# Feed-forward gate and up products by seven block products instead of eight

## The chip, the cores and the metric

The program runs on one core of one Trainium2 chip. Its time is the device time of one execution in microseconds (us). Engines: PE multiplies matrices (TensorE), ACT is ScalarE, DVE is VectorE, POOL is GpSimd, and SP is SyncE, whose queue issues nearly all DMAs here. PEld is PE's loading of weights, which runs beside its matmuls.

## The reference, cut to what matters

One layer of a hybrid decoder, for 1024 prompt tokens and 32 sample tokens (1056 in all), model width 1024, hidden width 2048, all in float32:

```
x += 1/2 * SwiGLU_1(rms(x))
x += W_out(sig(g_s5) * Up_s5(S5 branch) + sig(g_m) * Up_m(mLSTM branch))
x += 1/2 * SwiGLU_2(rms(x))
x += (p @ W_ple) * sigmoid(rms(x) @ W_ple_gate)
y  = rms(x) * g_final

SwiGLU(x) = (silu(x @ w_gate) * (x @ w_up)) @ w_down     # 1024 -> 2048 -> 1024
```

The change touches the two SwiGLU stages, called FFN1 and FFN2 here, and the places where x enters and leaves them.

## The kernel before, in words

Activations lie with features on the 128 partitions and the 1056 tokens along the free axis: x is 8 tiles of 128x1056. Tokens are taken in three chunks of 384, 384 and 288 (CH, L31), so that an accumulator fits a bank of PSUM. A float32 product is made of three matmuls in the type fp32r. Each factor is split into a high half (ACT rounds it, L87) and the rest (DVE subtracts, L88), and `mm3` (L101 to L106) adds high by high, high by low and low by high. `unit` (L108) is one accumulator: 24 matmuls for 8 feature tiles of 128.

An FFN (`ffn`, L246) goes over 16 tiles of 128 hidden features. For each, `gate_up` (L253) loads a 128-column piece of the gate and of the up weight (512 KB each, `weight`, L90), splits them, and makes three units of each. DVE multiplies the gate's unit by the 1/RMS of its token (`rb`, L262), ACT takes silu, DVE multiplies by `rb` and by the up unit, and the result is split into `hh` and `hl` (L268), which stay on chip. `down` (L270) takes groups of 4, 4, 4, 2 and 2 hidden tiles, with one further `gate_up` put ahead of each group so that PE has work while the last halves are split; its results are added to x on DVE (L279).

The RMS norm is folded: products run on x times gain. `norm` (L161) gives a hook, called once for each tile and chunk of x as it becomes final; the hook makes the two halves of x times gain (ACT L176, DVE L177), and the sums of squares come after it (L197, L198). `rstd` (L203) makes 1/RMS: two small PE products (L218, L235) with a power on POOL (L225) between.

Start of FFN1: `load_x` (L118) loads nine token tiles, transposes each with PE (`xT`, L155), takes it from PSUM on ACT or DVE (L139), and after the tiles 2, 5 and 8 calls the hook for one chunk. So the first chunk's products can begin after three token tiles. Start of FFN2: `join` (L1152) ends with a loop over chunks, and inside it over the 8 tiles (L1182): 6 matmuls (`mm_wo`), DVE's addition to x (L1175), and the hook.

The order of instructions on each engine is written by a scheduler that simulates them; each engine then runs its own list strictly in order, and waits on semaphores of others. Tiles come from pools with a fixed count of buffers (L39 to L49): 3 buffers for high halves of weights and 3 for low, 2 for raw weights, 16 + 8 + 10 large tiles for activations, and 4 + 4 banks of PSUM (`pmm`, `paux`).

Of the kernel before, what the change touches and what calls it, by code (L numbers as in the profile page):

```python
# [30 lines left out]
CH = ((0, 384), (384, 384), (768, 288))   # token chunks of a product  # L31


class Kernel:
    def __init__(self, tc, a, outs, ctx, dbg=None):
# [16 lines left out]
    def consts(self):  # L52
# [55 lines left out]
    def unit(self, w, xs, j, name, c=0, mw=P, aux=False):  # L108
        """One accumulator: products of all feature tiles for token chunk j."""
# [32 lines left out]
    def transpose_in(self, xp, xs, put, nf, name, pool, after=None, loaded=()):  # L142
        """put(feature tile, columns, PSUM tile) takes the tokens, transposed."""
        nc = self.nc
        for t in range(9):
# [4 lines left out]
            else:  # L150
                tt = pool.tile([P, NT if pool is self.ph else RW], F32, tag="h" if pool is self.ph else "r", name=f"{name}in{t}")[:n, :nf * P]
# [51 lines left out]
    def rstd(self, j, ss, rc, rb, name, cols=False):  # L203
        """1 / RMS of token chunk j, refined by one Newton step: columns [token, 128-token tile] and spread over the partitions."""
# [32 lines left out]

    def new_hl(self, n, name, lo="a"):
        lt = lambda k: (self.pa.tile([P, NT], F32R, tag="a", name=f"{name}l{k}") if lo == "a" else
                        self.px.tile([P, XW], F32R, tag="x", name=f"{name}l{k}")[:, :NT])  # L240
        return [(self.pa.tile([P, NT], F32R, tag="a", name=f"{name}h{k}"), lt(k)) for k in range(n)]

    def gate_up_weights(self, wg, wu, name, m):
        return [self.weight(w[:, m * P:(m + 1) * P], f"{name}{q}{m}") for q, w in (("g", wg), ("u", wu))]
# [1083 lines left out]
```

## Time and profile before

| | us |
|---|---|
| timed runs, median of 3 | 2344.37 |
| lowest and highest | 2341.33, 2345.77 |
| profiled execution, span from first to last instruction | 2343.1 |
| PE busy | 2310.0 (99%) |
| DVE busy | 1288.1 (55%) |
| ACT busy | 716.7 (31%) |
| POOL busy | 56.7 (2%) |

For the profiled execution only the span is given; it lies 1.3 us under the median and inside the range of the timed runs. A busy time is the union of an engine's instructions; successive matmuls overlap in the record, so the cost of one in a row of many is the distance from start to start and not its listed duration.

### The profile page before, as it was taken

Reading aid. Unit: us, or ns where it says so; the run is one execution under the profiler, and the core shown is the slowest. Engines: PE = TensorE matmul, PEld = TensorE weight load, DVE = VectorE, ACT = ScalarE, POOL = GpSimd, SP = SyncE. Lnnn points to the kernel's source line nnn. Section 1 sums busy time; section 2 is a strip of 40 time slices with the busy share of each in tenths; the row PEclk is TensorE's granted clock in tenths of the full one; section 3 lists DMA queues with packets and bytes.
Section 4 is the critical chain, followed back from the end, with each engine's and each line's share of the span. In section 5 each row is a group of like instructions: output and inputs, shape, how many; then the busy total and the mean of one; then the engine's idle time right before and its main releaser. Section 6 shows DMA issues by size and latency. Waiting matters only on the chain.

```text
span 2343.1 us, 36797 instructions
## 1 busy us (share of the span) xinstructions
PE 2310.0 (99%) x14895; PEld 2273.2 (97%) x14895; DVE 1288.1 (55%) x3101; ACT 716.7 (31%) x1332; POOL 56.7 (2%) x90
## 2 busy tenths in 40 slices
PE   8999999999999999999999899999999999999999
PEld 7999999999999999999999789999999999999998
DVE  6333333346868866868676377535533333334755
ACT  6111212114434433444344433213311111111543
POOL 0000000000001100000000000000000000000000
PEclk9999999999999999999999999999999999999999
DMA  4111111111444551222223488331111111111111
GB/s 136 39 55 37 55 37 55 46 46 42 141 117 132 138 141 39 60 59 62 52 76 97 138 275 279 100 129 46 55 37 55 36 55 37 55 37 59 56 37 74
DMA packets 254225, 188.37 MB, mean 80 GB/s; under 512 B 27052, under 2 KB 242060, under 8 KB 254056
## 3 DMA queue, kind: packets, MB, share of 16 engines
q1 hardware_dynamic: 234816, 164.43, 24.2%
q10 hardware_dynamic: 19240, 21.59, 2.7%
q8 instruction: 117, 1.92, 0.4%
q14 instruction: 52, 0.43, 0.1%
HBM read 142.09 MB, written 41.40 MB: 78 GB/s over the span
## 4 chain that ended last, share of the span: by engine, by line
PE 92%; DVE 4%; DMA 2%; issue 1%; ACT 1%; SPq 0%; DVEq 0%; ACTq 0%
PE mm_qk L104 3%; PE mm_f2g L105 3%; PE mm_f1g L105 3%; PE mm_qk L106 3%; PE mm_f2g L106 3%; PE mm_f2g L104 3%; PE mm_f2u L104 3%; PE mm_f1g L104 3%; PE mm_f1u L105 3%; PE mm_f1g L106 3%; PE mm_f2u L105 3%; PE mm_qk L105 3%; PE mm_f2u L106 3%; PE mm_f1u L106 3%; PE mm_f1u L104 3%; PE mm_f2d L104 2%
## 5 line engine op out<-in xcount | busy, mean ns | idle before, releaser
L104 PE MATMUL mm_qk<-n2h,wh_qk 128*128 128x384 f32 (+1 forms) x384 | 126.5, 329 | 0.0
L105 PE MATMUL mm_f1g<-n1l,wh_f1g 128*128 128x384 f32 (+1 forms) x384 | 125.9, 328 | 0.2 <-DVE n1l L177 0.2
L104 PE MATMUL mm_f2d<-f2hh,wh_f2d 128*128 128x384 f32 (+1 forms) x384 | 125.7, 327 | 0.3 <-DVE x L279 0.3
L106 PE MATMUL mm_qk<-n2h,wl_qk 128*128 128x384 f32 (+1 forms) x384 | 125.8, 328 | 0.0
L104 PE MATMUL mm_f1g<-n1h,wh_f1g 128*128 128x384 f32 (+1 forms) x384 | 125.5, 327 | 0.0
L105 PE MATMUL mm_f1u<-n1l,wh_f1u 128*128 128x384 f32 (+1 forms) x384 | 125.0, 325 | 0.0
L104 PE MATMUL mm_f1d<-f1hh,wh_f1d 128*128 128x384 f32 (+1 forms) x384 | 124.3, 324 | 0.4 <-DVE x L279 0.4
L104 PE MATMUL mm_f1u<-n1h,wh_f1u 128*128 128x384 f32 (+1 forms) x384 | 124.5, 324 | 0.0
L105 PE MATMUL mm_qk<-n2l,wh_qk 128*128 128x384 f32 (+1 forms) x384 | 124.4, 324 | 0.0
L106 PE MATMUL mm_f1u<-n1h,wl_f1u 128*128 128x384 f32 (+1 forms) x384 | 124.3, 324 | 0.0
L105 PE MATMUL mm_f2g<-n3l,wh_f2g 128*128 128x384 f32 (+1 forms) x384 | 124.2, 323 | 0.0
L106 PE MATMUL mm_f1g<-n1h,wl_f1g 128*128 128x384 f32 (+1 forms) x384 | 124.1, 323 | 0.0
L104 PE MATMUL mm_f2u<-n3h,wh_f2u 128*128 128x384 f32 (+1 forms) x384 | 124.0, 323 | 0.0
L105 PE MATMUL mm_f2d<-f2hl,wh_f2d 128*128 128x384 f32 (+1 forms) x384 | 124.0, 323 | 0.0
L105 PE MATMUL mm_f1d<-f1hl,wh_f1d 128*128 128x384 f32 (+1 forms) x384 | 124.0, 323 | 0.0
L106 PE MATMUL mm_f1d<-f1hh,wl_f1d 128*128 128x384 f32 (+1 forms) x384 | 123.9, 323 | 0.0
L105 PE MATMUL mm_f2u<-n3l,wh_f2u 128*128 128x384 f32 (+1 forms) x384 | 123.9, 323 | 0.0
L106 PE MATMUL mm_f2g<-n3h,wl_f2g 128*128 128x384 f32 (+1 forms) x384 | 123.9, 323 | 0.0
L106 PE MATMUL mm_f2u<-n3h,wl_f2u 128*128 128x384 f32 (+1 forms) x384 | 123.8, 322 | 0.0
L106 PE MATMUL mm_f2d<-f2hh,wl_f2d 128*128 128x384 f32 (+1 forms) x384 | 123.8, 322 | 0.0
L104 PE MATMUL mm_f2g<-n3h,wh_f2g 128*128 128x384 f32 (+1 forms) x384 | 123.6, 322 | 0.0
L279 DVE SCALAR_TENSOR_TENSOR x<-mm_f2d,x 128x384 f32<-128x384 f32 (+1 forms) x120 | 62.5, 523 | 88.8 <-PE mm_f2d L106 88.8
(628 smaller groups left out, 6826.1 us busy)
## 6 DMA issues: line engine op xcount, KB each, us to landing
wr_f1g<-in_w_gate_dram SPq DMA_DIRECT2D x16, 512.0 KB
wr_f1u<-in_w_up_dram SPq DMA_DIRECT2D x16, 512.0 KB
wr_f1d<-in_w_down_dram SPq DMA_DIRECT2D x16, 512.0 KB
wr_qk<-in_w_in_dram SPq DMA_DIRECT2D x16, 512.0 KB
c<-in_state_mlstm_c_dram SPq DMA_DIRECT2D x32, 256.0 KB
out_dram<-c ACTq DMA_DIRECT2D x32, 256.0 KB
wr_f2g<-in_w_gate_dram SPq DMA_DIRECT2D x16, 512.0 KB
wr_f2u<-in_w_up_dram SPq DMA_DIRECT2D x16, 512.0 KB
```

Source lines behind the costliest of these rows:

```text
L104: mm(ps, wh, xh, start=start, stop=False)
L105: mm(ps, wh, xl, start=False, stop=False)
L106: mm(ps, wl, xh, start=False, stop=stop)
L279: nc.vector.scalar_tensor_tensor(xs, ps, 0.5, xs, op0=ALU.mult, op1=ALU.add)
```

## The change

Gate and up are computed for 256 hidden columns at a time (8 steps `u`, each gate then up). The factors are cut into 2x2 blocks: the weight's 256 columns in two halves of 128 and its 8 feature tiles in two interleaved halves of 4 (even and odd tiles); x in even and odd tiles and two token halves of 528 (SH). Strassen's scheme in Winograd's form then needs seven block products, each over 4 feature tiles (12 matmuls), where the plain one needs eight. Each product is run for two column pieces of 264 tokens (SC).

- `forms`: for each pair of x tiles ACT makes x times gain (`fill`), POOL makes four sums or differences of 528 columns, in place over x's own tiles, and seven forms are split on ACT and DVE. 28 forms, each a tile that holds both halves, stay on chip for the whole FFN.
- `sweights`: for each 256 columns two raw loads, four additions on POOL (128x512), seven splits.
- `sproducts`: the seven products of a column piece in four accumulators (a, d from `pmm`, b, c from `paux`); ACT copies one to a temporary, DVE combines them, and `gate` or `up` takes the four blocks of the result. POOL does the multiplications by `rb` and by the gate.
- The hidden tiles are stored to DRAM (`d_h`) and loaded again for the down products, in groups of 8, 6 and 2. Because the forms overwrite x, x is stored to DRAM (`d_xs`) before and loaded again at the down products.
- `load_x` builds the forms after the ninth token tile. The last loop of `join` goes tile by tile instead of chunk by chunk, and the hook builds the forms of a pair when its second tile is final.
- The three pools of large tiles become one of 34, the weights' halves share 8 buffers, raw weights have 3 and the buffer for dynamic DMA descriptors is set to 512.

```
+    def forms(self, i, fill, tmp, name):
+        n = [self.pr.tile([P, RW], ...)[:, :NT] for q in "ab"]
+        fill(i, *n)
+        s = {"b11": n[0][:, :SH], "b21": n[1][:, :SH], "nb22": n[1][:, SH:]}
+        for j, q in enumerate(("t1", "t2", "t3", "t4")):
+            s[q] = tmp[j // 2][:, j % 2 * SH:(j % 2 + 1) * SH]
+        g.tensor_tensor(s["t3"], n[0][:, SH:], s["nb22"], ALU.add)
+        g.tensor_tensor(s["t1"], n[0][:, SH:], s["b11"], ALU.subtract)
+        g.tensor_tensor(s["t2"], s["nb22"], s["t1"], ALU.add)
+        g.tensor_tensor(s["t4"], s["b21"], s["t2"], ALU.add)
+        for q in self.FORMS:
+            f[q] = self.pa.tile([P, 2, SH], F32R, tag="s", name=f"{name}{q}_{i}")
+            self.split(s[q], f[q][:, 0], f[q][:, 1])
...
+    def sweights(self, src, name):
...
+        def form(q, src, add=None):
+            if add is not None:
+                g.tensor_tensor(src, src, add, ALU.add)
+            t = pw.tile([P, 2, 4, P], F32R, tag="w", name=f"w{q}_{name}")
+            self.split(src, t[:, 0], t[:, 1])
+        form("a11", a11)
+        form("s3", a11, a21)
+        form("s2", a11, a22)
+        form("s1", a21, a22)
+        form("a12", a12)
+        form("a22", a22)
+        form("s4", a12, a11)
...
+    def sproducts(self, W, F, c, name, put):
...
+        def product(ps, k, start):
+            for i, f in enumerate(F):
+                for j, (wq, xq) in enumerate(((0, 0), (0, 1), (1, 0))):
+                    nc.tensor.matmul(ps, w[:, wq, i], f[q][:, xq, cs], ...)
+        product(a, 0, True)
+        nc.scalar.copy(p1, a)
+        product(d, 1, True)
+        product(b, 2, True)
+        v.tensor_tensor(v2, b, p1, ALU.add)
+        v.tensor_tensor(w3, d, v2, ALU.subtract)
+        product(e, 3, True)
+        put(1, 1, e, w3, ALU.add)
+        product(a, 4, False)
+        put(0, 0, a, None, None)
+        product(d, 5, False)
+        put(1, 0, d, v2, ALU.subtract)
+        product(e, 6, False)
+        put(0, 1, v2, e, ALU.subtract)
...
+    def norm_s(self, g, name):
...
+        def fill(i, na, nb):
+            nc.scalar.activation(na, xa, AF.Copy, scale=ga)
+            nc.scalar.activation(nb[:, :SH], xb[:, :SH], AF.Copy, scale=gb)
+            nc.scalar.activation(nb[:, SH:], xb[:, SH:], AF.Copy, scale=nb_)
+        def build(i):
+            for m in (2 * i, 2 * i + 1):
+                nc.sync.dma_start(self.d_xs[m], self.x[m])
+            F.append(self.forms(i, fill, self.x[2 * i:2 * i + 2], name))
...
+        groups = ((0, 8), (8, 6), (14, 2))
+        self.x = None
+        for f, n in groups:
+            for m in range(f, f + n):
+                nc.sync.dma_start(h, d_h[m])
+                self.split(h, hh, hl)
+            if not f:
+                for m in range(KT):
+                    nc.sync.dma_start(self.x[m], self.d_xs[m])
...
-            if t in done:
-                for m in range(KT):
-                    hook(m, done[t])
+            if t == 8:
+                for i in range(4):
+                    build(i)
...
-        for j in range(3):
-            for m in range(KT):
+        for m in range(KT):
+            for j in range(3):
                 piece(ws[m // 4], mg[6:], m, m % 4, j)
-                hook(m, j)
+            hook(m)
```

**Place 1: PE at the start of FFN1.** `xT` are the transposes of token tiles, `mm_f1g` and `mm_f1u` the accumulators of gate and up, `n1h` and `n1l` the halves of x times gain. Before, around the last transposes of the third token tile:

```order
L155 MATMUL xT_6_195<-ident,xin_102 128x128
L104 MATMUL mm_f1g_0_492<-n1h_203,wh_f1g_239 128x384
L155 MATMUL xT_7_198<-ident,xin_102 128x128
L104 MATMUL mm_f1u_0_521<-n1h_203,wh_f1u_245 128x384
L155 MATMUL xT_0_251<-ident,xin_249 128x128
L105 MATMUL mm_f1g_0_492<-n1l_204,wh_f1g_239 128x384
L106 MATMUL mm_f1g_0_492<-n1h_203,wl_f1g_240 128x384
```

Now, from the last transpose of the ninth and last token tile (`nrb` spreads 1/RMS; `mma` to `mmd` are the four accumulators, the digit behind the step the column piece, `n1b` and `n1t` forms of x, with the pair's number behind them):

```order
L235 MATMUL xT_7_366<-ident,xin_343 128x32
L315 MATMUL nrb_n_507<-ident,rc_n_100 128x128 x3
L315 MATMUL nrb_n_520<-ident,rc_n_100 128x128 x3
L315 MATMUL nrb_n_535<-ident,rc_n_100 128x128 x2
L315 MATMUL nrb_n_535<-ident,rc_n_100 128x32
L183 MATMUL mma_f1g_0_572<-n1b_0_382,wa_f1g_547 128x264 x3
L183 MATMUL mmd_f1g_0_589<-n1t_0_385,ws_f1g_551 128x264
L183 MATMUL mma_f1g_1_685<-n1b_0_382,wa_f1g_547 128x264 x3
L183 MATMUL mmd_f1g_1_702<-n1t_0_385,ws_f1g_551 128x264
L183 MATMUL mmb_f1g_0_602<-n1t_0_388,ws_f1g_555 128x264
L183 MATMUL mmd_f1g_0_589<-n1t_0_385,ws_f1g_551 128x264 x2
```

Before, products stand between the transposes; now none stands before the last transpose and the spread of 1/RMS, and the first ones take turns over the accumulators as the forms of pair 0 come.

**Place 2: PE at the start of FFN2.** Before, from the end of the last `join` loop into the first gate product:

```order
L104 MATMUL mm_wo_2_2_16572<-mgh_14942,wh_wo_16280 128x288
L105 MATMUL mm_wo_2_2_16572<-mgl_14943,wh_wo_16280 128x288
L106 MATMUL mm_wo_2_2_16572<-mgh_14942,wl_wo_16281 128x288
L104 MATMUL mm_f2g_0_16678<-n3h_16292,wh_f2g_16666 128x384
L105 MATMUL mm_f2g_0_16678<-n3l_16293,wh_f2g_16666 128x384
```

Now, from the place where the sums of squares of the third and last chunk of tokens are taken (`nps`, behind the products that read the last pair's form `n3b_3`):

```order
L183 MATMUL mma_f2g_0_17808<-n3b_3_17714,wa_f2g_17798 128x264 x2
L183 MATMUL mma_f2g_1_17921<-n3b_3_17714,wa_f2g_17798 128x264 x2
L315 MATMUL nrb_n_17752<-ident,rc_n_15980 128x128 x3
L298 MATMUL nps_n_17757<-ones,rb_n_15979 128x2 x2
L298 MATMUL nps_n_17757<-ones,rb_n_15979 32x2
L315 MATMUL nrb_n_17771<-ident,rc_n_15980 128x128 x2
L315 MATMUL nrb_n_17771<-ident,rc_n_15980 128x32
L183 MATMUL mmb_f2g_0_17838<-n3t_0_17414,ws_f2g_17791 128x264 x3
L183 MATMUL mmb_f2g_0_17838<-n3t_1_17512,ws_f2g_17791 128x264 x3
```

Before, the first gate product follows the last `mm_wo` at once, and the norm comes under later products. Now PE's list holds only `mma` and `mmd` products between the last `mm_wo` and the whole norm, and every `mmb` and `mmc` stands behind the norm's last spread.

**Place 3: SP's queue at the change from the products to the down stage of FFN1.** `d_f1h` is the hidden tiles' place in DRAM, `f1hr` a hidden tile loaded again, `wr_f1d` raw down weights, `x_f` x loaded again. None of the stores and reloads has a row before.

```order
L398 DMA f1hr_4535<-d_f1h 128x1056
L100 DMA wr_f1d_5_4993<-in_w_down_dram 128x8x128
L389 DMA d_f1h<-f1h_4014 128x1056
L398 DMA f1hr_4541<-d_f1h 128x1056
L389 DMA d_f1h<-f1h_4013 128x1056
L100 DMA wr_f1d_6_5077<-in_w_down_dram 128x8x128
L398 DMA f1hr_4547<-d_f1h 128x1056
L398 DMA f1hr_4553<-d_f1h 128x1056
L404 DMA x_f_4557<-d_xs 128x1056
```

The stores of the last step's two hidden tiles stand ahead of the reloads of the sixth, seventh and eighth hidden tile, and these ahead of x.

## Rows read from the trace of the kernel before

**Rows 1.** The page's head: span, and busy time, share and instructions of each engine.
```profile
span 2343.1 us, 36797 instructions
...
PE 2310.0 (99%) x14895; PEld 2273.2 (97%) x14895; DVE 1288.1 (55%) x3101; ACT 716.7 (31%) x1332; POOL 56.7 (2%) x90
```

**Rows 2.** The longest of PE's waits: line, releaser: us in total, times, longest.
```profile
PE nnT L1050 <- DVE smA L1047: 9.5, 1, 9.5
```

**Rows 3.** The chain that ended last, share of the span by engine.
```profile
PE 92%; DVE 4%; DMA 2%; issue 1%; ACT 1%; SPq 0%; DVEq 0%; ACTq 0%
```

**Rows 4.** PE's timeline at four moments: start, duration, engine, line, operation.
```profile
199.96 0.34 PE L104 MATMUL mm_f1g<-n1h,wh_f1g 128*128 128x384 f32 x1
...
204.17 0.34 PE L104 MATMUL mm_f1u<-n1h,wh_f1u 128*128 128x384 f32 x1
...
1113.60 0.28 PE L868 MATMUL v2t<-wh_v,n2h 128*128 128x256 f32 x1
...
1115.96 0.28 PE L870 MATMUL v2t<-wh_v,n2l 128*128 128x256 f32 x1
```

**Rows 5.** Work of `mm_f1g`, then `mm_f1u`, in the first 60 us (count in brackets).
```profile
0.00:60.00 60.00, 24.84 (x99) 17.57 (x99) 2.12 (x4) 1.00 0.43 135
...
0.00:60.00 60.00, 21.23 (x89) 16.25 (x90) 1.56 (x3) 1.00 0.43 135
```

**Rows 6.** ACT's instructions by shape: count, busy us, mean ns; then idle time.
```profile
L197 ACT ACTIVATE sq_n<-x 128x384 f32<-128x384 f32 x42 | 21.8, 519 | 7.5 <-DVE ss_n L198 2.9 <-DVE nt_n L227 2.6 <-DVE nt_n L226 1.6
L87 ACT ACTIVATE wh_f1d<-wr_f1d 128x1024 fp32r<-128x1024 f32 x16 | 17.0, 1062 | 63.4 <-PE mm_f1d L105 41.1 <-issue 12.5 <-PE mm_f1g L105 9.9
...
L87 ACT ACTIVATE f1hh<-f1h 128x384 fp32r<-128x384 f32 x32 | 16.8, 526 | 113.7 <-DVE f1h L267 113.7
...
L176 ACT ACTIVATE n1h<-x,vecs 128x384 fp32r<-128x384 f32 x16 | 9.2, 611 | 0.0
...
L126 ACT ACTIVATE junk<-xin 128x1024 f32<-128x1024 f32 x8 | 8.5, 1060 | 2.4 <-DMA xin<-in_x_prompt_dram 2.2
L139 ACT COPY x<-xT 128x128 f32<-128x128 f32 x32 | 7.5, 260 | 6.9 <-PE xT L155 6.9
...
L87 ACT ACTIVATE wh_gt<-wr_gt 128x512 fp32r<-128x512 f32 x1 | 0.6, 634 | 1.8 <-issue 1.8
```

**Rows 7.** DVE's instructions by shape.
```profile
L198 DVE TENSOR_TENSOR ss_n<-ss_n,sq_n 128x384 f32<-128x384 f32 x42 | 23.3, 554 | 0.3
L88 DVE TENSOR_TENSOR wl_f1d<-wr_f1d,wh_f1d 128x1024 fp32r<-128x1024 f32 x16 | 19.6, 1226 | 8.8 <-ACT wh_f1d L87 8.8
...
L1175 DVE SCALAR_TENSOR_TENSOR x<-mm_wo,x 128x384 f32<-128x384 f32 x32 | 17.8, 557 | 31.3 <-PE mm_wo L106 31.3
...
L621 DVE TENSOR_TENSOR s5y<-S,s5x 128x256 f32<-128x256 f32 x8 | 3.4, 420 | 7.3 <-PE S L619 7.3
...
L88 DVE TENSOR_TENSOR wh_gt<-wr_gt,wh_gt 128x512 fp32r<-128x512 f32 x1 | 0.7, 692 | 0.1
```

**Rows 8.** POOL's instructions by shape.
```profile
L225 POOL TENSOR_TENSOR rc_n<-nv_n,mhalf 128x3 f32<-128x3 f32 x12 | 12.7, 1056 | 1423.1 <-DVE nv_n L221 833.9 <-ACT n4h L176 545.0 <-DVE nv_n L224 22.6
L582 POOL TENSOR_TENSOR s5y<-s5c,s5v 128x576 f32<-128x576 f32 x8 | 9.9, 1239 | 103.7 <-DMA s5x<-d_u 64.9 <-ACT s5x L576 14.4 <-DMA s5x<-d_k 12.4
```

**Rows 9.** Stretches: us, busy PE, PEld, DVE, ACT, POOL; PE's clock; DMA share; GB/s.
```profile
0.00:20.00 20.00, 12.81 (x44) 9.47 (x45) 9.95 (x37) 14.37 (x33) 2.86 (x18) 1.00 0.84 287
...
593.00:598.00 5.00, 5.00 (x33) 5.00 (x33) 4.97 (x15) 2.79 (x7) 0.00 (x0) 1.00 1.05 402
...
1330.00:1340.00 10.00, 4.46 (x20) 2.23 (x24) 2.56 (x7) 0.44 (x1) 0.00 (x0) 0.55 0.45 136
...
1630.00:1640.00 10.00, 10.00 (x68) 9.86 (x67) 10.00 (x22) 7.70 (x15) 0.00 (x0) 1.00 0.01 2
```

**Rows 10.** Timelines of POOL and DVE around 738 us.
```profile
737.26 1.22 POOL L582 TENSOR_TENSOR s5y<-s5c,s5v 128x576 f32<-128x576 f32 x1 [2.92 <-ACT s5x L576]
...
738.10 1.47 DVE L88 TENSOR_TENSOR wl_gm<-wr_gm,wh_gm 128x1024 fp32r<-128x1024 f32 x1 [0.76 <-ACT wh_gm L87]
```

More of the change, by code (lines that the diff above doesn't have):

```diff
@@ L81, in vectors @@
         self.gain = {n: vec[:, 8 * i:8 * i + 8] for i, n in enumerate(("g_ffn1", "g_mix", "g_ffn2", "g_ple", "g_mhead"))}
+        neg = pc.tile([P, 2, 8], F32, name="nvecs")
+        for i, n in enumerate(("g_ffn1", "g_ffn2")):
+            nc.vector.tensor_scalar(neg[:, i], self.gain[n], -1.0, None, op0=ALU.mult)
+            self.gain["-" + n] = neg[:, i]
         self.cw = vec[:, 40:104].rearrange("p (j t) -> p j t", j=4)
@@ new lines, in sweights @@
+    def sweights(self, src, name):
+        nc, pw, g, v = self.nc, self.pw, self.nc.gpsimd, self.nc.vector
+        A = []
+        for mh in range(2):
+            raw = pw.tile([P, KT, P], F32, tag="raw", name=f"wr{mh}_{name}", bufs=3)
+            nc.sync.dma_start(raw, src[:, mh * P:(mh + 1) * P].rearrange("(k p) m -> p k m", p=P))
+            A.append([raw.rearrange("p (i k) m -> p k i m", k=2)[:, kh] for kh in range(2)])
+        (a11, a12), (a21, a22) = A
+        out = []
+        def form(q, src, add=None):
[3 more added lines that the diff above has]
+            self.split(src, t[:, 0], t[:, 1])
+            out.append(t)
+        form("a11", a11)
[5 more added lines that the diff above has]
+        form("s4", a12, a11)
+        return out
@@ L122, in load_x @@
+    def load_x(self, build, st):
+        self.x = [self.px.tile([P, XW], F32, tag="s", name=f"x{m}")[:, :NT] for m in range(KT)]
         ss = self.pt.tile([P, 9], F32, tag="ssc", name="ssc", bufs=1)
-        def squares(t, tt):
-            junk = self.pr.tile([P, RW], F32, tag="r", name=f"junk{t}")[:tt.shape[0], :DM]
-            self.nc.scalar.activation(junk, tt, AF.Square, accum_out=ss[:tt.shape[0], t:t + 1])
         def after(t, tt):
@@ L150, in transpose_in @@
             else:
-                tt = pool.tile([P, NT if pool is self.ph else RW], F32, tag="h" if pool is self.ph else "r", name=f"{name}in{t}")[:n, :nf * P]
+                tt = pool.tile([P, XW if pool is self.ph else RW], F32, tag="s" if pool is self.ph else "r", name=f"{name}in{t}")[:n, :nf * P]
                 nc.sync.dma_start(tt, src)
@@ L236, in rstd @@
         nc.scalar.copy(rb[:, o:o + n], ps)
-    def new_hl(self, n, name, lo="a"):
[L239 to L244, printed above, removed]
@@ L292, in down @@
                         hook(m, j)
-        done = 0
-        for i, (f, n) in enumerate(groups):
-            while done < f + n:
-                gate_up(done)
-                done += 1
-            last = i == len(groups) - 1
-            if not last:
-                gate_up(done)
-                done += 1
-            elif before_last:
-                before_last()
-            down(f, n, last)
     def scratch(self):
@@ L849, in head_proj @@
         rb, rc = st["rb"], st["rc"]
-        q, k = ([self.ph.tile([P, NT], F32, tag="h", name=f"{n}{h}_{i}")[:, :NP] for i in range(2)] for n in "qk")
+        q, k = ([self.ph.tile([P, NT], F32, tag="s", name=f"{n}{h}_{i}")[:, :NP] for i in range(2)] for n in "qk")
         for i in range(2):
@@ L1139, in gated_heads @@
         for k in ks:
[L1140 to L1141 removed]
+            hl = [self.pa.tile([P, NT], F32R, tag="s", name=f"hm{q}{k}") for q in "hl"]
             self.hm.append(hl)
[L1143 removed]
+            f1 = self.px.tile([P, XW], F32, tag="s", name=f"hm{k}")[:, :NT]
             f2 = self.pr.tile([P, RW], F32, tag="r", name=f"to{k}")[:, :NT]
@@ L1166, in join @@
                 self.split(t, mg[m][0][:, o:o + n], mg[m][1][:, o:o + n])
-        self.x = [self.pa.tile([P, NT], F32, tag="a", name=f"x2_{m}") for m in range(KT)]
+        self.x = [self.pa.tile([P, NT], F32, tag="s", name=f"x2_{m}") for m in range(KT)]
         for m in range(KT):
@@ L1221, in output @@
         v.tensor_copy(gain, ps)
-        ss = [self.ph.tile([P, NT], F32, tag="h", name=f"fss{j}")[:, :CH[j][1]] for j in range(3)]
+        ss = [self.ph.tile([P, NT], F32, tag="s", name=f"fss{j}")[:, :CH[j][1]] for j in range(3)]
         def hook(m, j):
```

192 lines of the change are left out of this document (120 added, 72 removed).

## The prediction

> **What bounds the kernel now.** I read the page's head first: PE is busy 2310.0 of 2343.1 us, DVE 55%, ACT 31%, POOL 2% [rows 1]. Then PE's waits: only some 33 us of the span are without a matmul, and the longest single wait is 9.5 us, far from the feed-forward stages [rows 2]. The chain of waits says the same: 92% of what ended last is PE [rows 3]. So the time is the number of matmuls times their spacing, and a change pays if it takes matmul columns away and keeps PE fed. The spacing comes from PE's timeline [rows 4]: 24 matmuls of 384 columns lie between 199.96 and 204.17 us, 175.4 ns each, and 20 of 256 columns between 1113.60 and 1115.96 us, 118.0 ns each. That is 0.448 ns for each further column. By interpolation 288 columns cost 132.4 ns and the new 264 columns 121.6 ns. No row has 264 columns; 118.0 and 132.4 bound it.
>
> Two places then decide what else happens: the starts of the two stages. At the first, PE does 188 feed-forward matmuls by 60 us [rows 5]. 144 of them are the six units of hidden tile 0, 24 x (2 x 175.4 + 132.4) ns x 2 = 23.2 us, and 44 more at 175.4 ns are 7.7 us. So 29.1 us of the first 60 are start cost. At the second, PE is busy 10.00 of 10 us from 1630 to 1640 while DVE is full too and ACT is at 7.7 [rows 9]: PE has no idle time there, but the engines that prepare its data have no room.
>
> **The products: what is removed.** Now each FFN makes 32 triples of units, 11.60 us each: 371.1 us. After, it makes 8 steps x gate and up x 2 pieces x 7 products x 12 = 2688 matmuls of 264 columns: 326.9 us. Saved: 44.2 us per FFN, 88.4 us in all. At the bounds of the spacing (118.0 and 132.4 ns) it is 107.8 or 30.4; I keep the interpolation, since both ends lie on one line with 384, and allow 5 us.
>
> **The steady state.** For 256 hidden columns of one weight PE needs 168 x 121.6 ns = 20.4 us. In that time the weight's forms need four additions on POOL and seven splits. POOL's 128x576 addition took 1.239 us [rows 8]; in proportion 512 columns are 1.10 us and 264 are 0.57. A split of 128x512 took 0.634 us on ACT [rows 6] and 0.692 on DVE [rows 7]. For a step u (two weights, 40.9 us) DVE has 14 splits, 9.7 us, and 24 operations on PSUM at about 0.43 (the row with 256 columns has 0.420): 20 us, 49%. ACT has 14 splits and 12 small operations, some 14 us. POOL has 8 additions, 8.8 us, and 20 multiplications, 11.4 us: 20 us, 49%. PE stays the bound; I cost this at nothing. The cover is gone when one weight's chain exceeds 20.4 us (third rival).
>
> **Start of FFN1.** Before, products begin after three token tiles; now after nine and their forms [place 1 of the change]. Until x is complete ACT has 9 squares of 1.06 us, 32 copies of 0.26 and 8 weight splits of 0.634 [rows 6], 23 us after the first landing near 4 us, and SP brings nine token tiles and three raw weights, 5.9 MB, which at 287 GB/s [rows 9] is 20.5 us. With the waits between them I take 33 us (27 to 38). Then ACT alone must make the forms. Its scaled copy of 384 columns took 0.611 us, and from 634 and 1062 ns for 512 and 1024 columns each further column is 0.836 ns: 4 copies of 1056 at 1.17, 8 of 528 at 0.73, 28 splits at 0.65 make 28.7 us; three spreads of `rb` and six weight splits make 5.3; waits for POOL's first sums some 2. The last form is ready near 69 us. PE by then can have done the accumulators of four products as the forms come, about 120 matmuls, 14.6 us. Start cost 54.4 us against 29.1: a loss of 25 (15 to 35).
>
> **Start of FFN2.** From the beginning of the last `join` loop DVE has 24 additions to x (16 at 0.557, 8 at about 0.46), 21 additions of squares (14 at 0.554, 7 at about 0.45), 28 splits of 528 columns at 0.71 and seven weight splits at 0.692 [rows 7]: 12.6 + 10.9 + 19.9 + 4.8 = 48.2 us. ACT has 24 squares (16 at 0.519, 8 at about 0.44), the 12 fills, 28 splits and seven weight splits: 11.8 + 10.6 + 18.1 + 4.4 = 44.9. PE meanwhile has 144 matmuls of `mm_wo`, 23.2 us, and the products into accumulators a and d alone, 72 matmuls, 8.8 us, because its list holds every b and c product behind the norm [place 2]. The norm's tail is a power on POOL, 1.06 us [rows 8], some small steps on DVE, a product and a copy: 4 us after the last sum. 48.2 + 4 - 32.0 = 20 us of idle PE where there was none. Bounds 10 and 30.
>
> **The hidden tiles through DRAM.** The last two are stored only when POOL has multiplied them; SP's queue holds the reloads of the sixth to eighth tile behind these stores [place 3]. Two stores, three reloads (541 KB each) and a weight are 3.2 MB, 8 us at 402 GB/s, the rate of the stores of x now [rows 9]; with 1.2 us on ACT and 1.25 on DVE for the last split (by the 1024-column rows) about 11 us after the last product. PE has the parts of four accumulators that use the first five tiles, 60 matmuls at a mean of 161 ns, 9.7 us. Left: some 3 us per FFN (0 to 12), 6 in all. x comes behind in the same queue; the first addition to x waits for it, and PE then has four banks' worth more. The later groups of 6 and 2 hidden tiles need buffers that the group before frees: 1 us at each of four borders (0 to 3), 4 in all.
>
> **The clock.** From 1330 to 1340 us PE was busy 4.46 of 10 us and its granted clock fell to 0.55 [rows 9], the lower of the levels 1.2 and 2.4 GHz for most of that stretch. Each of the new idle stretches at the starts can cost a few us at the lower level when PE comes back: 4 us (0 to 12).
>
> **The sum.** -88.4 + 25 + 20 + 6 + 4 + 4 = -29 us. The mixer keeps its order around the matmuls; its buffers come from the shared pool, for which I take 0 and allow 10 both ways. Against the profiled execution: 2343.1 - 29 = 2314. The median of the timed runs is 1.3 us higher, so **2315 us**.
>
> **First rival: the starts are hidden better.** If the scheduler's order lets PE eat the forms as they come and both starts together cost 25 instead of 45, and handovers, borders and clock 5 instead of 14, the gain is 58: 2286 us. For it: ACT and DVE work on different forms at once, and PE only needs one pair's forms at a time. Against: both lists are nearly full in my sums, and the b and c products stand behind the norm. Chance 0.20.
>
> **Second rival: POOL and DVE exclude each other.** While POOL's addition ran from 737.26 to 738.48, DVE's split began at 738.10 and took 1.47 us instead of 1.226 [rows 7, 10]: 0.24 us longer for 0.38 us of overlap. If that holds all along, 16 additions of 528 columns (1.14 us, 18 us) and 28 splits (19.9 us) of one FFN go one after the other: 38 us where ACT needs 34 at the first start (4 more), and 48.2 + 18 at the second (18 more). 2315 + 22 = 2337 us. The steady state would still fit: 20 + 9.7 us in 40.9. Against: one overlapping pair is thin, and the additions fall partly into DVE's gaps. Chance 0.13.
>
> The Trainium skill, "SBUF — State Buffer" (section "SBUF: two separate sides"), says that a GpSimd operation and a VectorE operation with two SBUF inputs take the shared ports as an exclusive lock, and the later one blocks fully. By that rule this rival holds; the trace's one pair agrees with it in direction, 0.24 us of 0.38.
>
> **Third rival, slower: a weight's chain is longer than its products.** The seven forms of a weight are made in place, addition and split in turn. Strictly in series that is 4 x 1.10 + 7 x (0.634 + 0.692) = 13.7 us, and POOL's ten multiplications for the same 20.4 us of PE put up to 5.7 between: 19.4. It decides above 20.4. With POOL's and DVE's steps a fifth longer (1.47 for 1.226) the chain is 22.5 to 23.3; half of the excess of 2.9, over 32 weights, is 46 us: 2360 us, the whole of it 2407. For it: POOL goes from 2% to half. Against: eight weight buffers let a chain begin half a step ahead. Chance 0.14.
>
> **Fourth rival: DRAM at the handover.** If the queue's reloads and x are late by the upper bounds, 12 us at each change of stage and 3 at each border, 22 and 8 come instead of 6 and 4, and the clock takes 12: 2315 + 28 = 2343 us, no change that can be told. Chance 0.10.
>
> **How the numbers follow.** My forecast holds with 0.43, from 2300 to 2332 by its own bounds. A measurement of this kernel can tell about 0.2%, 4.7 us, from no change. Faster than 2339.7: 0.43 + 0.20, two thirds of 0.13 and a third of 0.10: 0.75. Within: the rest of the second rival and some of the fourth, 0.08. Slower: the third and the last part of the fourth, 0.17. The range of 8 in 10 goes from 2284 (first rival) into the lower part of the third, 2355.
>
> **What would show it.** Right: matmuls of 264 columns 121 to 122 ns apart; PE's rows in the first 70 us some 25 us emptier than now; 15 to 25 us of waits on DVE or ACT around the end of `mm_wo`; almost no waits of PE in `mma` to `mmd` in between. The second rival would show in splits of 0.71 us stretched towards 1.3 beside POOL; the third in PE waiting for weight forms in each step; the fourth in PE's waits for `f1hh` or in additions to x that wait for DMA. The forecast is wrong if the products' spacing is off the line, if these waits come in every step, or if the starts cost under 30 us or over 65 together.

## The result and the profile after

The changed kernel takes 2326.25 us (median of 4, 2323.53 to 2326.41) against 2345.07 before: ratio 0.9919, 95% interval 0.9905 to 0.9933. It is faster by 19 us where 29 were forecast; the time is inside the range (2284 to 2355) and inside the forecast's own bounds (2300 to 2332), 11 us above the forecast. The profiled execution has a span of 2324.7 us, 18.4 less than [rows 1]. The page's head answers to those rows:

```profile
span 2324.7 us, 39749 instructions
...
PE 2252.8 (97%) x15663; PEld 2206.2 (95%) x15663; DVE 1394.2 (60%) x3211; ACT 823.7 (35%) x1560; POOL 549.1 (24%) x570
...
PE 88%; DVE 6%; DMA 2%; issue 1%; ACT 1%; POOL 1%; SPq 1%; DVEq 0%; ACTq 0%; POOLq 0%
```

PE's busy time fell by 57 us and the span by 18: PE's share of the chain fell from 92% [rows 3] to 88%, DVE's rose from 4% to 6%, and POOL came in with 1%. PE's waits (line, releaser: us, times, longest) say where:

```profile
PE vT L79 <- DMA vrows<-in_conv_b_dram: 8.0, 1, 8.0
PE mma_f2g L183 <- DVE n3b L93: 7.6, 3, 5.2
PE mmd_f1g L183 <- ACT n1t L92: 6.2, 3, 2.6
PE nnT L1173 <- DVE smA L1170: 4.8, 1, 4.8
```

The second and third are forms that come late, at the starts of FFN2 and FFN1. The fourth is [rows 2], halved. The first, PE's wait for the small vector loads (`vrows`) behind its first token tile, no step of the prediction had.

The products run as forecast. PE's timeline in the middle of FFN1 groups 12 matmuls in a row:

```profile
199.74 1.63 PE L183 MATMUL mmd_f1g<-n1t,ws_f1g 128*128 128x264 f32 x12
201.21 1.64 PE L183 MATMUL mmb_f1g<-n1t,ws_f1g 128*128 128x264 f32 x12
202.69 1.63 PE L183 MATMUL mmc_f1g<-n1t,ws_f1g 128*128 128x264 f32 x12
204.16 1.63 PE L183 MATMUL mma_f1g<-n1b,wa_f1g 128*128 128x264 f32 x12
205.63 0.64 PE L183 MATMUL mma_f1u<-n1b,wa_f1u 128*128 128x264 f32 x4
```

48 matmuls from 199.74 to 205.63 us are 122.7 ns each; the interpolation from [rows 4] had given 121.6. In the stretches below (columns as in [rows 9]) the row from 200 us shows PE full in the steady state. In the others, at the two starts, PE has gaps and a granted clock of 0.50 to 0.65 while DVE, ACT and POOL work:

```profile
50.00:60.00 10.00, 6.26 (x24) 5.12 (x24) 6.66 (x8) 6.33 (x11) 5.97 (x4) 0.65 0.00 0
60.00:70.00 10.00, 6.75 (x24) 5.52 (x24) 6.66 (x8) 6.34 (x11) 5.96 (x4) 0.50 0.00 1
...
200.00:250.00 50.00, 50.00 (x413) 50.00 (x412) 27.34 (x48) 17.25 (x35) 34.46 (x35) 1.00 0.21 65
...
1640.00:1650.00 10.00, 2.12 (x7) 1.44 (x6) 9.61 (x12) 4.85 (x10) 5.63 (x5) 0.51 0.12 38
1650.00:1660.00 10.00, 5.97 (x25) 5.36 (x25) 7.96 (x16) 7.59 (x14) 5.18 (x5) 0.50 0.00 1
```

From 50 to 60 and from 60 to 70 us every number nearly repeats: one pair of x tiles is made into forms in 10 us, although no engine is busy over 6.8 of them. From 1640 to 1650 us, at the second start, DVE is nearly full with 9.61.

To see where the 18.4 us are, the span is cut at PE's instructions: the last down product of FFN1, the first and last `mm_wo`, the last down product of FFN2. Two such cuts, of one tile each (count: shortest, median, longest in ns, then the first and last start in us), for the kernel before:

```profile
L106 PE MATMUL mm_f1d<-f1hh,wl_f1d x384: 288/336/343, 145.5 to 587.0; 128*128 128x384 f32 x128, 128*128 128x288 f32 x64
...
L104 PE MATMUL mm_wo<-mgh,wh_wo x96: 290/337/397, 1548.5 to 1642.0; 128*128 128x384 f32 x64, 128*128 128x288 f32 x32
```

and after:

```profile
L111 PE MATMUL mm_f1d<-f1hh,wl_f1d x384: 290/335/525, 390.1 to 584.2; 128*128 128x384 f32 x126, 128*128 128x288 f32 x66
...
L109 PE MATMUL mm_wo<-mgh,wh_wo x96: 290/336/445, 1534.8 to 1631.6; 128*128 128x384 f32 x64, 128*128 128x288 f32 x32
```

The mixer between them takes 961.5 us before and 950.6 after, although the change does not touch its arithmetic. Among its waits before was a second one, of 5.0 us, beside [rows 2]:

```profile
PE hT L902 <- DVE mlC L897: 5.0, 1, 5.0
```

This wait is gone after. All kernels of this study, cut in the same way (us, each from one profiled execution):

| kernel | FFN1 | mixer | join | FFN2 | rest | span |
|---|---|---|---|---|---|---|
| before | 587.0 | 961.5 | 93.8 | 562.8 | 138.0 | 2343.1 |
| after | 584.2 | 950.6 | 97.1 | 554.4 | 138.4 | 2324.7 |
| e1 pools alone | 595.8 | 948.9 | 94.0 | 563.2 | 137.8 | 2339.7 |
| e2 work tiles | 581.7 | 947.8 | 100.9 | 555.9 | 137.7 | 2324.0 |
| e3 sums on DVE | 576.7 | 950.9 | 97.1 | 552.6 | 137.9 | 2315.2 |
| e4 late norm | 586.1 | 947.7 | 98.9 | 545.0 | 138.0 | 2315.7 |
| e5 small loads first | 581.7 | 947.1 | 97.5 | 553.6 | 138.0 | 2317.9 |
| e6 pools, small loads first | 592.6 | 948.5 | 93.8 | 563.1 | 137.8 | 2335.8 |
| e7 three edits | 574.9 | 948.5 | 96.9 | 545.3 | 137.7 | 2303.3 |
| e8 three edits, work tiles | 573.2 | 949.0 | 97.7 | 544.7 | 138.3 | 2302.9 |
| e9 busy PE | 579.4 | 950.3 | 96.9 | 548.1 | 137.8 | 2312.5 |

FFN1 gave 2.8 us and FFN2 8.4; the join lost 3.3 and the rest 0.4; the mixer gave 10.9. All ten kernels with the new pools have a mixer of 947 to 951 us.

### The profile page after: what moved, and what is told of

It reads as the page before. It is cut to its first block, busy times and chain, and to the rows that moved or that the text cites. A ratio compares the mean times of both kernels' runs of the same rounds, so it can differ in the third digit from the quotient of the medians.

```text
span 2324.7 us, 39749 instructions
## 1 busy us (share of the span) xinstructions
PE 2252.8 (97%) x15663; PEld 2206.2 (95%) x15663; DVE 1394.2 (60%) x3211; ACT 823.7 (35%) x1560; POOL 549.1 (24%) x570
## 4 chain that ended last, share of the span: by engine, by line
PE 88%; DVE 6%; DMA 2%; issue 1%; ACT 1%; POOL 1%; SPq 1%; DVEq 0%; ACTq 0%; POOLq 0%
PE mm_qk L110 3%; PE mm_qk L109 3%; PE mm_qk L111 3%; PE mm_f2d L110 2%; PE mm_f1d L110 2%; PE mm_f2d L111 2%; PE mm_f1d L111 2%; PE mm_f2d L109 2%; PE mm_f1d L109 2%; PE mmc_f2g L183 2%; PE mmc_f2u L183 2%; PE mmd_f2u L183 2%; PE mmd_f1u L183 2%; PE mma_f2u L183 2%; PE mma_f1u L183 2%; PE mmc_f1u L183 2%
## 5 line engine op out<-in xcount | busy, mean ns | idle before, releaser
L415 DVE SCALAR_TENSOR_TENSOR x_f<-mm_f1d,x_f 128x384 f32<-128x384 f32 (+1 forms) x72 | 37.0, 520 | 88.0 <-PE mm_f1d L111 87.7
L956 DVE SCALAR_TENSOR_TENSOR cv<-raw,vecs,cv 128x384 f32<-128x384 f32 (+1 forms) x144 | 84.8, 589 | 7.3 <-ACT cv L954 6.1
L415 DVE SCALAR_TENSOR_TENSOR x_f<-mm_f2d,x_f 128x384 f32<-128x384 f32 (+1 forms) x72 | 37.1, 520 | 85.6 <-PE mm_f2d L111 85.6
L109 PEld LDWEIGHTS mm_f1d<-f1hh,wh_f1d 128*128 128x128 f32 x384 | 72.4, 189 | 3.3 <-DVE x_f L415 1.7
L109 PEld LDWEIGHTS mm_f2d<-f2hh,wh_f2d 128*128 128x128 f32 x384 | 71.7, 188 | 2.9 <-ACT f2hh L92 2.1
L110 PEld LDWEIGHTS mm_f2d<-f2hl,wh_f2d 128*128 128x128 f32 x384 | 72.1, 188 | 1.3 <-DVE f2hl L93 1.3
L110 PEld LDWEIGHTS mm_f1d<-f1hl,wh_f1d 128*128 128x128 f32 x384 | 72.7, 189 | 0.6 <-DVE f1hl L93 0.6
L111 PEld LDWEIGHTS mm_f1d<-f1hh,wl_f1d 128*128 128x128 f32 x384 | 72.7, 189 | 0.0
L110 PEld LDWEIGHTS mm_qk<-n2l,wh_qk 128*128 128x128 f32 x384 | 72.3, 188 | 0.1
L111 PEld LDWEIGHTS mm_qk<-n2h,wl_qk 128*128 128x128 f32 x384 | 72.2, 188 | 0.1
```

The lines of the kernel that those rows point to most:

```text
L109: mm(ps, wh, xh, start=start, stop=False)
L110: mm(ps, wh, xl, start=False, stop=False)
L111: mm(ps, wl, xh, start=False, stop=stop)
L415: v.scalar_tensor_tensor(xs, ps, 0.5, xs, op0=ALU.mult, op1=ALU.add)
L956: v.scalar_tensor_tensor(acc, raw[:, o + i:o + i + wd], self.cw[:, i, T:T + 1], acc, op0=ALU.mult, op1=ALU.add)
```

## The experiments

Theories: the two starts lost what the products gained, by the buffers of the forms (e2), by POOL and DVE in each other's way (e3), by the b and c products behind the norm (e4), or by the late small loads (e5); and the mixer's gain is the pools' (e1, e6). An edit also lets the scheduler write the whole order anew, so a difference of 3 us in a stretch that the edit does not touch is not read as its effect.

**e1, the pools alone.** The kernel before with plain products and the change's pools:

```
-        self.pw = pool("wts", 3)
-        self.pa = pool("pa", 16)
-        self.px = pool("px", 8)
-        self.ph = pool("ph", 10)
+        self.pw = pool("wts", 8)
+        self.pa = self.px = self.ph = pool("slots", 34)
...
-        raw = pw.tile([P, ko, mc], F32, tag="raw", name="wr_" + name, bufs=2)
+        raw = pw.tile([P, ko, mc], F32, tag="raw", name="wr_" + name, bufs=3)
...
-    nc = _bacc.Bacc("TRN2", target_bir_lowering=False, num_devices=1)
+    nc = _bacc.Bacc("TRN2", target_bir_lowering=False, num_devices=1, dynamic_dma_scratch_size=512)
```

> The kernel before with the pools alone as in the change: one pool of 34 large tiles, 8 shared weight halves, 3 raw weights, the descriptor buffer of 512; plain gate and up products. In the changed kernel's trace the stretch between the last down product of FFN1 and the first product with w_m_up's successor w_out is 950.4 us against 961.3 before, with PE's waits for hT 0.7 (5.0 before) and nnT 4.8 (9.5 before). Theory A (these 10.9 us come from the pools, not from the block products): the time falls by 7 to 11 us, to 2334 to 2338, with the hT and nnT waits as in the changed kernel, and the block products themselves are worth only about 10 us. Theory B (they come from the new order of work around the mixer): the time stays within 3 us of 2345.

Measured: 2343.16 us, ratio 0.9998 (0.9989 to 1.0007). The total says theory B, the stretches say otherwise: the mixer takes 948.9 us, 12.6 less than before, and FFN1 8.8 more (the profiled execution, of 2341.46 us, lies 1.7 under the median). Its waits:

```profile
PE vT L76 <- DMA vrows<-in_conv_b_dram: 9.0, 1, 9.0
...
PE nnT L1048 <- DVE smA L1045: 3.2, 1, 3.2
```

With the pools the small loads stand behind weights in SP's queue, and PE waits 9.0 us for them; nnT's wait fell from 9.5 [rows 2] to 3.2, and the wait for `hT` is gone. Two effects of one edit seem to cancel; e6 tests it.

**e2, other work tiles.** The two work tiles of a pair come from the pool of 34:

```
-        n = [self.pr.tile([P, RW], F32, tag="r", name=f"{name}n{q}_{i}")[:, :NT] for q in "ab"]
+        n = [self.pa.tile([P, XW], F32, tag="s", name=f"{name}n{q}_{i}")[:, :NT] for q in "ab"]
```

> The changed kernel with the two work tiles of the forms (x times gain of a pair) taken from the pool of 34 instead of two buffers of their own, so that the next pair's fills need not wait for this pair's last splits. In the changed kernel a pair takes 10 us (forms from 39 to 78 us) though ACT is busy only 6.3 and DVE 6.7 of 10. Theory A (the starts lose time because the pairs go in series through two buffers): a pair falls to 7 to 8 us, FFN1's start shortens by 6 to 10 us, FFN2's by 3 to 8, total 2310 to 2317. Theory B (POOL's additions and DVE's splits keep each other waiting, so that more buffers do not help): under 3 us.

Measured: 2324.34 us, ratio 0.9918 (0.9904 to 0.9931), the changed kernel's. Theory A falls. In the changed kernel ACT waits 6.0 us in all for the last splits of the pair before (`n1nb`); here it does not, and the fills of the last two pairs start 9.0 us apart instead of 9.9. But the last product of FFN1 starts only 0.6 us earlier (394.2 instead of 394.8 us). Theory B's condition, under 3 us, is met; its reason is tested by e3.

**e3, the sums of the forms on DVE.**

```
-        g.tensor_tensor(s["t3"], n[0][:, SH:], s["nb22"], ALU.add)
+        v.tensor_tensor(s["t3"], n[0][:, SH:], s["nb22"], ALU.add)
```

and so for t1, t2 and t4.

> The changed kernel with the 16 sums of forms of each FFN on DVE instead of POOL. A sum of 528 columns takes 1.30 to 1.79 us on POOL, and splits on DVE beside them 1.1 to 1.8 us instead of 0.70. Theory A (the two engines exclude each other and POOL is slow): the sums take 0.70 us each, splits fall to 0.70, a pair falls from 10 to about 8 us, FFN1's start is 6 to 8 us shorter; at FFN2, where DVE is full, the gain is smaller, 0 to 6; total 2313 to 2321. Theory B (the two buffers set the pace whoever adds): within 3 us of 2326. If DVE's load decides at FFN2, that start gets longer by up to 11 us, since 16 sums of 0.70 are added to a full engine.

Measured: 2314.68 us, ratio 0.9874 (0.9859 to 0.9889). Theory A, in the faster half of its range. The span is 9.5 us shorter than the changed kernel's; FFN1 gives 7.5 of them, FFN2 1.8. POOL's and DVE's timelines in the changed kernel show why:

```profile
51.26 1.30 POOL L135 TENSOR_TENSOR x<-n1na,n1nb 128x528 f32<-128x528 f32 x1 [2.04 <-ACT n1nb L328]
52.52 1.31 POOL L137 TENSOR_TENSOR x<-n1nb,x 128x528 f32<-128x528 f32 x1
53.90 1.66 POOL L138 TENSOR_TENSOR x<-n1nb,x 128x528 f32<-128x528 f32 x1
55.52 1.79 POOL L136 TENSOR_TENSOR x<-n1na 128x528 f32<-128x528 f32 x1
```

```profile
53.27 1.12 DVE L93 TENSOR_TENSOR n1t<-x,n1t 128x528 fp32r<-128x528 f32 x1 [2.86 <-ACT n1t L92]
54.86 3.01 DVE L93 TENSOR_TENSOR n1t<-x,n1t 128x528 fp32r<-128x528 f32 x2 [0.48 <-ACT n1t L92]
57.79 0.70 DVE L93 TENSOR_TENSOR n1b<-n1nb,n1b 128x528 fp32r<-128x528 f32 x1
```

POOL's first sum has DVE idle and takes 1.30 us; beside DVE's splits the sums take 1.66 and 1.79. DVE's splits take 1.12 us and then 3.01 for two, and 0.70 once POOL is done. The lengthenings are near the overlaps: the split of 53.27 is 0.42 us over its 0.70, and the sum before it still had 0.56 us to go; the sum of 53.90 is 0.36 us over its 1.30, and that split still had 0.49 us to go. By shape, the changed kernel (count, busy us, mean ns):

```profile
L93 DVE TENSOR_TENSOR n1t<-x,n1t 128x528 fp32r<-128x528 f32 x16 | 17.5, 1125 | 10.0 <-ACT n1t L92 10.0
```

and e3:

```profile
L93 DVE TENSOR_TENSOR n1t<-x,n1t 128x528 fp32r<-128x528 f32 x16 | 11.8, 770 | 0.7 <-ACT n1t L92 0.6
...
L135 DVE TENSOR_TENSOR x<-n1na,n1nb 128x528 f32<-128x528 f32 x4 | 2.8, 707 | 1.6 <-ACT n1nb L328 1.6
```

The same split takes 1.125 us with the sums on POOL and 0.770 with them on DVE, and a sum 0.707 instead of 1.30 to 1.79. The Trainium skill, "SBUF — State Buffer" (section "SBUF: two separate sides"), says that a VectorE operation with two SBUF inputs and a GpSimd operation that reads SBUF take their shared ports as an exclusive lock, so that the later one waits; these rows agree with it, since the later one is longer by about the overlap. How much of FFN1's gain is the lock and how much POOL's slower sum is not separated.

Why FFN2 gives only 1.8 us stands in DVE's rows from the first product of the last `join` loop to the end of the norm's last spread (columns of the first line as in [rows 9]; then count, busy us, mean ns), in the changed kernel:

```profile
1604.38:1673.11 68.73, 47.02 (x255) 41.93 (x253) 61.42 (x100) 42.28 (x77) 34.08 (x23) 0.81 0.22 83
...
L93 DVE TENSOR_TENSOR n3t<-x,n3t 128x528 fp32r<-128x528 f32 x16 | 16.1, 1022 | 0.0
L343 DVE TENSOR_TENSOR rb_n<-rb_n,sq_n 128x384 f32<-128x384 f32 x14 | 14.0, 1004 | 0.4 <-ACT sq_n L342 0.4
```

and in e3:

```profile
1597.17:1664.65 67.48, 46.68 (x255) 41.86 (x253) 59.20 (x116) 42.29 (x77) 14.09 (x7) 0.82 0.23 84
...
L93 DVE TENSOR_TENSOR n3t<-x,n3t 128x528 fp32r<-128x528 f32 x16 | 12.0, 768 | 0.0
L343 DVE TENSOR_TENSOR rb_n<-rb_n,sq_n 128x384 f32<-128x384 f32 x14 | 7.7, 552 | 0.0
```

DVE is busy 61.4 us beside POOL's 16 sums and 59.2 us when it makes them itself. Here, where DVE is full, handing the sums to POOL saved DVE nothing: its other operations grew by about what the sums cost it in e3 (16 at 0.70 to 0.97 us).

**e4, the norm of FFN2 behind its first use.**

```
-                for j, (o, n) in enumerate(CH):
-                    self.rstd(j, st["rb"][:, o:o + n], st["rc"], st["rb"], name)
+                st["late"] = [lambda j=j, o=o, n=n: self.rstd(j, st["rb"][:, o:o + n], st["rc"], st["rb"], name) for j, (o, n) in enumerate(CH)]
...
             def gate(mh, nh, x, y, op):
+                for f in st.pop("late", ()):
+                    f()
```

> The changed kernel with the norm of FFN2 (sums over partitions, power, spread) issued at the first use of its result instead of before the products, so that accumulators b and c of the first column piece no longer stand behind it in PE's list. Theory A (b and c behind the norm cost PE work at the start): products with b and c fill part of the idle time, up to 48 matmuls of 122 ns or 5.9 us, total 2319 to 2323. Theory B (the forms themselves are late, so PE only does the same work in another order): within 2 us of 2326.

Measured: 2317.69 us, ratio 0.9890 (0.9876 to 0.9903). Theory A, and beyond it. FFN2 is 9.4 us shorter and the join before it 1.8 longer (6 products now stand ahead of the last `mm_wo`), so 7.6 in the two, more than theory A's 5.9. From 1660 us on PE is nearly full in e4, where the changed kernel still has 2 us of gaps to 1670 and a slow stretch behind:

```profile
1660.00:1670.00 10.00, 9.75 (x60) 9.54 (x61) 9.83 (x19) 5.80 (x10) 5.04 (x4) 0.73 0.10 28
1670.00:1680.00 10.00, 10.00 (x83) 9.84 (x82) 4.91 (x14) 3.09 (x7) 4.88 (x6) 1.00 0.00 1
```

and the changed kernel:

```profile
1660.00:1670.00 10.00, 7.84 (x47) 7.32 (x47) 9.10 (x17) 5.03 (x10) 5.89 (x5) 0.80 0.09 26
1670.00:1680.00 10.00, 8.64 (x46) 8.39 (x47) 2.49 (x9) 2.42 (x4) 1.17 (x2) 0.66 0.01 2
```

In 1670 to 1680 PE does 83 matmuls instead of 46. Of the b and c matmuls of the first gate step 24 start before 1670 us, where the changed kernel has none, and the norm's tail no longer holds up the rest. What the theory did not have is the granted clock, which is 1.00 in this stretch instead of 0.66. In the changed kernel PE stands still for 2.1 us before the norm's last spread, and of the products behind it the first 24 take longer than the next 12:

```profile
1673.04 3.01 PE L183 MATMUL mmb_f2g<-n3t,ws_f2g 128*128 128x264 f32 x12
1675.85 2.45 PE L183 MATMUL mmc_f2g<-n3t,ws_f2g 128*128 128x264 f32 x12
1678.13 1.63 PE L183 MATMUL mmb_f2g<-n3t,ws_f2g 128*128 128x264 f32 x12
```

The 24 take 5.09 us, where 122.7 ns each would be 2.94: some 2 us at the lower clock, an estimate from these rows. No run separates them from the order.

**e5, the small loads first.** `vrows` is loaded in `consts`, behind the first three token tiles:

```
             nc.sync.dma_start(self.xin[t], a["x_prompt"][0][t * P:(t + 1) * P])
+        rows = self.vrows = self.ph.tile([P, NT], F32, tag="s", name="vrows")[:120, :P]
+        srcs = [a[n][0] for n in ("g_ffn1", "g_mix", "g_ffn2", "g_ple", "g_mhead")]
+        for n, g in enumerate(srcs):
+            nc.sync.dma_start(rows[8 * n:8 * n + 8], g.rearrange("(k p) -> k p", p=P))
...
-        rows = self.ph.tile([P, NT], F32, tag="s", name="vrows")[:120, :P]
+        rows = self.vrows
```

> The changed kernel with the small loads of the per-feature vectors (vrows) put right behind the first three token tiles in SP's queue, as they stood before the change; in the changed kernel they come behind three weights and four small loads, and PE waits 8.0 us for them before its second token tile (1.6 us before the change). Theory A (this wait delays the forms and so all of FFN1): FFN1's first product and the time come 5 to 8 us earlier, 2318 to 2321. Theory B (the token tiles or ACT would be late anyway): within 2 us of 2326.

Measured: 2320.08 us, ratio 0.9899 (0.9885 to 0.9912). The total fits theory A, its path does not: FFN1 is only 2.5 us shorter, and the mixer, which the edit does not touch, 3.5. The last transpose starts at 29.9 instead of 37.0 us, but the weight sums now come between the sums of the forms on POOL, three of them from 37 to 57 us; two in its timeline:

```profile
50.64 1.75 POOL L159 TENSOR_TENSOR wr_f1u<-wr_f1u,wr_f1u 128x512 f32<-128x512 f32 x1
52.35 1.77 POOL L139 TENSOR_TENSOR x<-n1nb,x 128x528 f32<-128x528 f32 x1
54.08 1.79 POOL L137 TENSOR_TENSOR x<-n1na 128x528 f32<-128x528 f32 x1
55.83 1.73 POOL L159 TENSOR_TENSOR wr_f1u<-wr_f1u 128x512 f32<-128x512 f32 x1
```

The last split of a form starts at 81.0 us on DVE, against 82.1 in the changed kernel: x came 7 us earlier and the last form 1.

**e6, the pools with the small loads first.** e1 with the edit of e5.

> The pools alone (plain products, as in e1) with the same order of the small loads. In e1 the stretch from the last down product of FFN1 to the first output product of the mixer was 948.9 us against 961.5 before, but FFN1 ended 8.8 us later, with a wait of 9.0 us for the small loads. Theory A (the pools' change moves two things that cancel: the mixer gains 12 us, the late small loads cost 9): 2332 to 2337, clearly faster than before. Theory B (the late end of FFN1 is something else, or the mixer's gain hangs on it): within 3 us of 2344.

Measured: 2339.10 us, ratio 0.9979 (0.9971 to 0.9988): faster than before, by less than theory A. FFN1 comes back by 3.2 us of the 8.8, the mixer keeps its 13. So the mixer's gain is that of the regrouping (pools, raw weights, descriptor buffer) and not the products'. What the other 5.6 us of FFN1 are is open; in e6 the granted clock is 0.66 from 30 to 40 us, with 41 matmuls, where the kernel before has 1.00 and 61.

**e7, the three edits together; e8, with e2's work tiles too.** The changed kernel with the diffs of e3, e4 and e5, and then with that of e2.

> The changed kernel with the three edits together: sums of forms on DVE (alone 11.6 us faster than the changed kernel), the norm of FFN2 behind its first use (alone 8.6), small loads first (5 to 8 expected). If they act on different waits the time is 2326 less 25 to 28: 2298 to 2301. If two of them take away the same wait (sums and norm both at FFN2), 2302 to 2308.

Measured: 2305.26 us, ratio 0.9841 (0.9827 to 0.9854), faster than both kernels, and inside the second forecast: 21.0 us less than the changed kernel, where the three alone add up to 26.4. In FFN2 the three give 9.1 us together, where e4 alone gave 9.4 and e3 alone 1.8; so it is there that the edits overlap.

> As e7, and the two work tiles of the forms from the pool of 34 as in e2. There it was worth 2 us with POOL and DVE in each other's way; theory A (with the sums on DVE, the two buffers are next in line): 3 to 8 us faster than e7; theory B (ACT and DVE are now the pace, each busy 8 to 9 of 10 us in the forms): within 2 us of e7.

Measured: 2305.28 us, ratio 0.9836 (0.9822 to 0.9849). Theory B: the two buffers do not bind the total.

**e9, PE kept busy in the starts.** e7 with matmuls of zero weights between:

```
                     nc.tensor.matmul(ps, w[:, wq, i], f[q][:, xq, cs], ...)
+                    if extra and k < 4 and i < n - 1:
+                        nc.tensor.matmul(ps, self.zero.to_broadcast([P, P]), f[q][:, xq, cs], start=False, stop=False)
```

> As e7, and behind every matmul of the first four products of the first gate step (of the pairs 0 to 2, both column pieces, both FFNs) one more into the same accumulator with zero weights, 72 for each FFN, which adds nothing to the result. In e7 the granted clock is 0.67 from 40 to 60 us and 0.50 to 0.59 from 1630 to 1650 us, where PE waits between the forms. Theory A (the lower clock in the starts costs time: matmuls at half speed when the last forms are there): with PE busier the granted clock stays higher, and the time falls by 3 to 8 us to 2297 to 2302. Theory B (the forms set the pace and the clock is only a sign of the waits): within 2 us of 2305, or up to 6 us slower, since 72 matmuls are 8.8 us of PE at full clock and part of them falls where PE has no time left.

Measured: 2314.06 us, ratio 0.9871 (0.9854 to 0.9887). The stretch from 50 us in e7:

```profile
50.00:60.00 10.00, 7.10 (x32) 6.46 (x33) 9.15 (x16) 8.45 (x15) 0.00 (x0) 0.67 0.00 0
```

and in e9:

```profile
50.00:60.00 10.00, 8.49 (x59) 8.08 (x60) 9.15 (x15) 8.46 (x16) 0.00 (x0) 0.90 0.01 2
```

The clock rose from 0.67 to 0.90, and the products of FFN1 ended no earlier (the last one starts at 387.2 us, 386.8 in e7). Theory A falls, and for this start theory B holds: the forms set the pace, and the clock is a sign of the waits. The total is 9 us slower, more than theory B's 6. The loss lies later: FFN1's down stage 4 (where the wait of `mm_f1d` for a split hidden tile grew from 1.1 to 3.1), FFN2 3, mixer 2; why is open. For the second start this run decides nothing.

## Why the prediction was right in sign and range, and where it was off

- **The products**: 5376 matmuls at 122.7 ns are 659.6 us. Saved 82.6, 88.4 forecast; the spacing was 1 ns off.
- **The steady state**: right that it costs nothing, PE 50.00 of 50. The loads were mis-sized: POOL's 264-column multiplication takes 0.863 us on average, not the 0.57 taken in proportion from [rows 8] (a multiplication of 576 columns, which the prediction calls an addition), so POOL is busy 34 of 50 us and not half. The third rival did not come.
- **Start of FFN1**, a term too small, though inside its bounds. The products end near 395.0 us (the last one starts at 394.84). Less 329.8 of products and 2.3 of 13 down products among them, the start cost 62.8 us; 54.4 were forecast. Against 29.1 before, 34 were lost instead of 25. The last transpose of x starts at 37.0 us and its last copy ends at 39.0, not at 33, and a pair took 10 us, since sums and splits stretch each other (e3); the prediction had ACT as the pace.
- **Start of FFN2**, the term that failed, beyond its bounds of 10 and 30. From the last `mm_wo` to the start of the last product 364.3 us pass where 329.8 and 2.3 of work lie: 32 lost, and 3.3 more in the join. 35 instead of 20. In the sum 48.2 + 4 - 32.0 the wrong number is DVE's 48.2: from the first product of the last `join` loop to the end of the norm's last spread 68.7 us pass instead of 52.2, and DVE is busy 61.4 of them. Beside POOL's sums its splits of `n3t` take 1.022 us instead of 0.71 and its sums of squares 1.004 instead of 0.554; in e3, without POOL's sums, they take 0.768 and 0.552. 68.7 - 32.0 is 36.7, near the 35 lost. That b and c products stand behind the norm was in the sum, which counted only a and d as work; e4 shows that another order gives back 7.6 us, with the clock in it.
- **The hidden tiles through DRAM, borders, clock**: 14 forecast. FFN1's down stage lost about 5 us more than before; FFN2's lost 7, where before the whole of FFN2 lost 6. So 6 are left. For the handover the working gives 11 - 9.7 = 1.3 us, and the forecast took 3 without a reason for the rest; the fourth rival's 22 and 8 would by its own bounds be 24 and 12, and its time 2349 instead of 2343. The clock fell; e9 found nothing to gain from it at the first start, and at the second the rows beside e4 put some 2 us on it, which the 35 contain.
- **The mixer**: taken as 0 with 10 both ways; it gave 10.9, and e1 and e6 show that it is the regrouping's. nnT's wait fell from 9.5 to 4.8 us and that for `hT`, 5.0, is gone; which of the pools does it was not tried.

The sum is then -82.6 + 34 + 35 + 6 - 11 = -19. The failed term is the starts, 45 forecast and 69 measured. The prediction had named "over 65 together" as a sign that it is wrong: by its own sign it failed there, although the time lies in its range. The second rival had put 22 us more on the starts, 67, and 2337 us, and its mechanism is what the rows show (e3). The mixer gave 11 back, which every case had at 0. The nearness of 2315 to 2326 is thus partly luck, two errors of opposite sign.

Against the same pools and loads (e6, 2339.10), the block products with better starts (e7, 2305.26) are worth 34 us of the 83 that the matmuls save.

## What to carry to other kernels

A saving in matmul work is paid for at the moments when PE has nothing else to do: find the start of the stage, list what each engine must make there, and count which engines slow each other down. Sums on POOL are not free beside DVE's splits: at FFN2's start they cost DVE as much time as making them itself. And work in PE's queue that waits for a late norm holds up all products behind it. When a change also regroups buffers, run the regrouping alone, and read its stretches and not only its total.

## What was not expected of the hardware

Half the columns cost POOL more than half the time: a sum of 528 columns took 1.30 us with DVE idle, and a multiplication of 264 columns 0.745 us at its shortest and 0.863 on average, beside DVE work (count: shortest, median, longest in ns):

```profile
L371 POOL TENSOR_TENSOR f1sg<-f1sg,rb_n x48: 745/759/1212, 84.8 to 375.1; 128x264 f32<-128x264 f32 x48
```

DVE's split of 528 columns took 0.70 us alone and 1.125 on average beside POOL's sums. A granted clock of 0.67 instead of 0.90 cost nothing where PE waits for data anyway, at the first start; at the second, where products were ready behind the norm, 24 of them took 5.09 us at the lower clock instead of 2.94.
